# Raw weights of the down projection in three rings, and a reordered last norm, in a one-core decoder layer

## The chip, the core and the metric

The kernel runs on one core of a Trainium2 chip. TensorE (PE) multiplies matrices and takes its stationary operand by a separate weight load (PEld); VectorE (DVE) and ScalarE (ACT) work on tiles element by element; GpSimd (POOL) does little here; SyncE (SP) issues the transfers. The engines run at the same time, each its own instructions in a fixed order, and wait for one another by semaphores. The metric is the device time of one execution in microseconds (us): 1220.66 us is the median of three executions of the kernel before.

## What is computed

One layer of a decoder with two mixers side by side: a gated delta rule with four heads, and dilated sliding-window attention with eight heads; then one output projection, a residual, and a gated MLP with a short causal convolution. The sequence has 1024 positions, the model width is 1024, the MLP width 2816. Only the end of it bears on this change:

```python
x = x + jnp.concatenate([o_a, o_b], axis=-1) @ w_out
h = rmsnorm(x, norm2_w)
u = causal_dwconv(h @ w_up, ffn_conv_w)
gate, up = u[..., :D_FF], u[..., D_FF:]
x = x + (jax.nn.silu(gate) * up) @ w_down
...
return rmsnorm(x, final_norm_w)

def rmsnorm(x, w):
    y = xf * lax.rsqrt(jnp.mean(xf * xf, axis=-1, keepdims=True) + EPS)
    return (y * w.astype(jnp.float32)).astype(x.dtype)
```

The kernel holds x transposed: 1024 features as eight tiles of 128 partitions, positions along the free axis. A mean over features is therefore a sum over the eight tiles and over the partitions.

## The kernel before

**Products.** Operands are split in a high and a low part of a reduced-width float32 type (`F32R`), and every product of 128x128 by 512 is three matrix multiplications (`mm3`: high by high, high by low, low by high). The high part is an ACT copy, the low part a DVE subtraction (`split_block`).

**The MLP.** `mlp_up` runs over 22 channel tiles n. Both projections use a recursive scheme with seven products in place of eight (`up_product`, P1 to P7 on the way up). Between products ACT copies partial sums out of the bank `pa` while PE goes on adding to it: `p1`, then `u2` (a tile of the ring `wlo`), then `u3`, then `xu`. The activation of each channel tile is stored in DRAM (`upark`).

**The down projection** (`mlp_down`, and `prep` for operands) has four stages of eleven steps j. A step of stages 0, 1 and 2 has two operand pairs (e = 0 on the four banks `pa`, e = 1 on the four banks `pb`), 24 multiplications of 512 columns; a step of stage 3 has one pair on `pa`, 12 multiplications. When a stage ends, DVE adds its eight finished banks to the residual tiles `x1h` (`add_to`, table `ADDS`), while PE already starts on the same banks for the next stage; a bank can be written again only when its add is done. The `pa` banks come first in each step, then `pb`. From stage 2's end on, `complete` squares finished rows on ACT and sums the squares of the eight tiles into `rstdB` on DVE.

`prep` for a step issues the loads of raw weights (`wd`, 512 KB, or `wa`, 256 KB) and of activations (`r1`, `r2`, from `upark`), combines them on DVE and splits them. The raw tiles lie in pools named by a tag, a ring of two buffers each:

| stage | raw weights in | others |
|---|---|---|
| 0 | `wst` and `whi` in turn | |
| 1 | `wd` in `wst`, `wa` in `whi` | `t2` (a difference of activations) in `wlo` |
| 2 | `wst` and `whi` | |
| 3 | `wst` and `whi` in turn | |

The split operands (`pr`) go round eleven tags. All transfers of the kernel are issued by SP, in one order. In the up projection `wst` and `whi` hold raw up weights and `wlo` holds `u2`.

**The tail.** The last five steps of stage 3 are done bank by bank in two halves of 256 positions (`last_product(i, sl)`): four left banks, then the right banks. `final_norm` makes the last norm of a part: multiplications of `rstdB` with ones sum over partitions (`ss`), a scalar operation, a power on POOL (`rsqrt`), transpositions that spread the result over partitions (`pb`), and eight DVE multiplications, each followed by a store of a tile. The norm of the left half is started behind the first right bank; its eight multiplications stand on DVE ahead of the adds of the last two right banks.

**What sets the order.** The order on PE is written out: the generators of a `Weave` yield until their operands are ready by a cost estimate, and each product gets a token that keeps the order. On the other engines a scheduler orders instructions by priorities and estimated times; `uv` and `ua` are DVE and ACT at raised priority, `after(inst, anchor)` forces one instruction behind another. So another ring or another wait can move DVE, ACT and SP instructions that the diff doesn't touch. In the compiled kernels the order on PE and POOL is the same but for the added products, and those of DVE, ACT and SP differ from the end of the up projection on.

In the profile L139 is the helper through which all engine operations but products pass, L189 the multiplications of `mm`, L193 the transpositions of `tp`.

Of the kernel before, what the change touches and what calls it, by code (L numbers as in the profile page):

```python
# [7 lines left out]
F32 = mybir.dt.float32  # L8
F32R = mybir.dt.float32r
AF = mybir.ActivationFunctionType  # L10
OP = mybir.AluOpType
# [4 lines left out]
P = 128  # L16
# [8 lines left out]
EPS = 1e-6  # L25
# [119 lines left out]
def hybrid_layer(tc, I, out):  # L145
    nc = tc.nc
    wv = Weave()
    ve = Engine(wv, nc.vector, "vector", 0.07, 0.00105)
    ac = Engine(wv, nc.scalar, "scalar", 0.12, 0.00085)

    uv = Engine(wv, nc.vector, "vector", 0.07, 0.00105, first=tc.high_priority)
    ua = Engine(wv, nc.scalar, "scalar", 0.12, 0.00085, first=tc.high_priority)
    po_ = Engine(wv, nc.gpsimd, "gpsimd", 0.15, 0.0021)
    sy = Engine(wv, nc.sync, "sync", 0.05, 0.00142, 2.2)
    es = ExitStack()
    cp = es.enter_context(tc.tile_pool(name="cp", bufs=1))
# [6 lines left out]
    def tile_(pool, shape, dt, name, tag, bufs):  # L163
        return wv.slot(pool.tile(list(shape), dt, name=name, tag=tag, bufs=bufs), tag, bufs)
# [20 lines left out]
    def after(inst, anchor, reason="keeps a slot free until it is needed"):  # L185
        tc.add_manual_dep(inst.ins, anchor.ins.name, order, reason=reason)

    def mm(dst, lhs, rhs, us, start=True, stop=True, **kw):
        tc.stamp_issue_order_token(nc.tensor.matmul(dst, lhs, rhs, start=start, stop=stop, **kw).ins, TOKEN)  # L189
        wv.product(us, dst, lhs, rhs)  # L190

    def tp(dst, src, idt=None, us=0.11):
        tc.stamp_issue_order_token(nc.tensor.transpose(dst, src, ident if idt is None else idt).ins, TOKEN)  # L193
        wv.product(us, dst, src)
# [43 lines left out]
    def rsqrt(dst, src, n):  # L238
        po_.tensor_tensor(dst, src, mhalf[:, :n], op=OP.pow)
# [14 lines left out]
    def bank(tag, name="ps"):  # L254
        return tile_(pp_, (P, 512), F32, name, tag, 2)
# [1094 lines left out]
    pcount = [0]  # L1350
    LAST = 5

    def raw_tile(name, tag, src, n=2):
        t = tile_(wp, [P, n, 512], F32, name, tag, 2)
# [29 lines left out]
    def prep(stage, j):  # L1384
        if stage == 0:

            g = raw_tile("wd", ("wst", "whi")[j % 2], wd_rows(j, 0))
            r = R1[j] = acts("r1", R1TAGS[j], j, 0)
            ops[stage, j] = list(zip(split_pair(g), split_pair(r)))
            q = R2[j] = A("r2", R2TAGS[j], shape=(P, 2, 512))  # L1390
            sy.dma_start(q[:, 0, :], upark[j][:, half(1)])
            ve.tensor_tensor(r[:, 0, :], q[:, 0, :], r[:, 0, :], op=OP.subtract)
        elif stage == 1:

            u = raw_tile("wd", "wst", wd_rows(j, 1))
# [5 lines left out]
            ve.tensor_tensor(u[:, 0, :], u[:, 1, :], a[:, 0, :], op=OP.subtract)  # L1401
            ve.tensor_tensor(t2, q[:, 1, :], r[:, 0, :], op=OP.subtract)
            w = split_pair(u)
            ops[stage, j] = [(w[0], split_one(t2)), (w[1], split_one(r[:, 0, :]))]
            ve.tensor_tensor(r[:, 1, :], r[:, 1, :], t2, op=OP.subtract)
        elif stage == 2:

            g = raw_tile("wd", "wst", wd_rows(j, 0))
            u = raw_tile("wd", "whi", wd_rows(j, 1))
            ve.tensor_tensor(g, g, u, op=OP.subtract)  # L1410
            ve.tensor_tensor(g[:, 1, :], g[:, 0, :], g[:, 1, :], op=OP.add)
            r = R2[j]
            ve.tensor_tensor(r[:, 0, :], r[:, 1, :], r[:, 0, :], op=OP.subtract)
            ops[stage, j] = list(zip(split_pair(g), split_pair(r)))
        else:

            a = raw_tile("wa", ("wst", "whi")[j % 2], wd_rows(j, 1)[:, 1:2], 1)
# [13 lines left out]
    def part(m, hh, sl):  # L1431
        return slice(512 * hh + sl.start, 512 * hh + sl.stop)

    def add_to(pd, m, hh, sl):
        x = x1h[m][:, part(m, hh, sl)]
        ve.tensor_tensor(x, x, pd[:, sl], op=OP.add)

    def complete(m, hh, sl):

        sp_ = part(m, hh, sl)  # L1440
        x = x1h[m][:, sp_]
        sq = tile_(sp, [P, 512], F32, "sq3", "t2", 2)
        ac.activation(sq[:, sl] if m else rstdB[:, sp_], x, AF.Square)
        if m:
            ve.tensor_tensor(rstdB[:, sp_], rstdB[:, sp_], sq[:, sl], op=OP.add)

    def final_norm(hh, sl, tags, between=None):
        n_ = (sl.stop - sl.start) // P
        ss = bank(tags[0])
        for c in range(n_):  # L1450
            o = 512 * hh + sl.start + c * P
            mm(ss[:, c:c + 1], rstdB[:, o:o + P], ones[:, :1], 0.215)
        rs = tile_(sp, [P, 4], F32, "rs3", "rs3", 2)
        ve.tensor_scalar(rs[:, :n_], ss[:, :n_], 1.0 / 1024, EPS, op0=OP.mult, op1=OP.add)
        rsqrt(rs[:, :n_], rs[:, :n_], n_)
        if between is not None:
            between()
        pb = bank(tags[1])
        for c in range(n_):
            tp(pb[:, c * P:(c + 1) * P], rs[:, c:c + 1].to_broadcast([P, P]))  # L1460
        for m in range(8):
            x = x1h[m][:, part(m, hh, sl)]
            ve.scalar_tensor_tensor(x, x, fw[:, m:m + 1], pb[:, :sl.stop - sl.start], op0=OP.mult, op1=OP.mult)
            sy.dma_start(out[m * P:(m + 1) * P, part(m, hh, sl)], x)
# [6 lines left out]
    def mlp_down():  # L1471
        yield from wv.until("up")
        whole = slice(0, 512)
        pa = [bank(t, "dw") for t in ("asc", "atr") for _ in range(2)]
        pb = [bank(t, "dw") for t in ("hf", "ch") for _ in range(2)]
        def down_step(stage, j):
            for e, (op, pds) in enumerate(zip(ops[stage, j], (pa, pb))):
                for i in range(4):
                    down(pds[i], i, op, whole, j == 0 and (stage == 0 or (stage, e) == (1, 1)), j == HT - 1)
                if j == HT - 1:  # L1480
                    mg, hh = ADDS[stage][e]
                    for i in range(4):
                        add_to(pds[i], 4 * mg + i, hh, whole)
                        if stage == 0 and e == 1:
                            complete(i, 0, whole)
                        if stage == 2 and e == 1:
                            complete(i, 1, whole)
                    if stage == 2 and e == 1:
                        for i in range(4):
                            complete(4 + i, 1, whole)  # L1490

        for n, (stage, j) in enumerate(STEPS):
            if n + 1 < len(STEPS):
                prep(*STEPS[n + 1])
            if n in XLOADS:
                load_x1(*XLOADS[n])
            if stage == 3 and j == HT - LAST - 1:
                final_norm(1, whole, ("hf", "ch"), lambda: down_step(stage, j))
            elif stage < 3 or j < HT - LAST:
                down_step(stage, j)  # L1500

        def last_product(i, sl):
            for j in range(HT - LAST, HT):
                down(pa[i], i, ops[3, j][0], sl, False, j == HT - 1)
            add_to(pa[i], 4 + i, 0, sl)
            complete(4 + i, 0, sl)
# [12 lines left out]
    wv.add(1, gates())  # L1519
# [69 lines left out]
```

## Time and profile before

| what | us |
|---|---|
| median of three executions | 1220.66 (1220.21 to 1220.72) |
| the profiled execution, whole | 1219.28 |
| its span, first to last instruction | 1217.5 |
| PE busy | 1200.4 |
| DVE busy | 946.1 |
| ACT busy | 574.6 |

Mean granted TensorE clock in the profiled execution: 0.996 of full speed. In the time lines a row gives the start, the duration, the engine, the line, the operation with output and inputs, the count of merged instructions, and in brackets the idle time ahead and what ended it. A row of waits gives the total, the number and the longest. A row of a windows table for one engine gives the stretch, its length, the busy time, the granted clock, the share of the DMA engines and GB/s; without a choice of engine it has busy times for PE, PEld, DVE, ACT and POOL in this order. A row of DMA issues gives the count, the size and the us from issue to landing; the row of one tensor's instructions gives the shortest, median and longest issue in ns.

### The profile page before, as it was taken

The numbers are of one execution on the slowest core, as the hardware profiler recorded it, in microseconds if no ns is written. First come the engines' busy times: TensorE is split into PE (matmuls) and PEld (weight loads), VectorE is DVE, ScalarE is ACT, GpSimd is POOL, SyncE is SP. The second block draws the span as 40 slices with busy tenths as digits, with TensorE's granted clock in tenths as the row PEclk, the third lists the DMA queues.
The fourth block names the chain that finished last, engine by engine and source line by source line (L and its number), as shares of the span: only waits on it lengthen the run. The fifth ranks groups of instructions, "written<-read, shape, count | busy, mean of one in ns | idle before, by whom it ended". The sixth has DMA issues, their size and how long they took to land.

```text
span 1217.5 us, 18285 instructions
## 1 busy us (share of the span) xinstructions
PE 1200.4 (99%) x7064; PEld 986.3 (81%) x7064; DVE 946.1 (78%) x1459; ACT 574.6 (47%) x1124; POOL 52.1 (4%) x46
## 2 busy tenths in 40 slices
PE   9999999999999999999999999999999999999996
PEld 7878887889777778888888888888888888787886
DVE  7675965566477686767989988989889889899875
ACT  7393344356344453655544544445444444344441
POOL 0311010003100000000000000000000000000000
PEclk9999999999999999999999999999999999999998
DMA  7425252335634213444213223132231496555623
GB/s 231 107 79 165 83 145 85 116 127 164 214 102 129 88 36 107 173 139 144 82 57 105 68 88 104 52 104 68 89 104 53 141 376 234 165 177 177 181 87 139
DMA packets 85799, 154.81 MB, mean 127 GB/s; under 512 B 21168, under 2 KB 36304, under 8 KB 85712
## 3 DMA queue, kind: packets, MB, share of 16 engines
q1 hardware_dynamic: 85712, 153.64, 39.4%
q8 instruction: 55, 0.90, 0.3%
q14 instruction: 32, 0.26, 0.1%
HBM read 117.68 MB, written 35.93 MB: 126 GB/s over the span
## 4 chain that ended last, share of the span: by engine, by line
PE 87%; DVE 6%; DMA 3%; issue 2%; ACT 2%; SPq 0%; POOLq 0%; POOL 0%; DVEq 0%; ACTq 0%
PE ps L189 44%; PE pa L189 20%; PE pc L189 10%; PE dw L189 10%; PE ps L193 3%; DMA wd<-in_wd 2%; DVE pr L139 2%; DVE x1h L139 1%; DVE wd L139 1%; DVE kT L139 1%; ACT dec L139 1%; PE warm L189 1%; DVE wlo L139 0%; DMA r<-upark 0%; ACT sq L141 0%
## 5 line engine op out<-in xcount | busy, mean ns | idle before, releaser
L189 PE MATMUL dw<-pr 128*128 128x512 f32 (+1 forms) x984 | 213.0, 377 | 2.2 <-DVE x1h L139 2.2
L189 PEld LDWEIGHTS dw<-pr 128*128 128x128 f32 x984 | 176.1, 188 | 38.0 <-DVE x1h L139 4.4
L189 PE MATMUL ps<-xhi,whi 128*128 128x512 f32 x384 | 158.5, 413 | 0.0
L189 PE MATMUL ps<-xhi,wlo 128*128 128x512 f32 x384 | 150.3, 391 | 0.0
L189 PE MATMUL ps<-xlo,whi 128*128 128x512 f32 x384 | 150.1, 391 | 0.0
L189 PE MATMUL pa<-T,pair 128*128 128x512 f32 x528 | 127.1, 389 | 0.0
L189 PEld LDWEIGHTS pa<-T,pair 128*128 128x128 f32 x528 | 99.0, 188 | 20.5
L189 PEld LDWEIGHTS ps<-xhi,wlo 128*128 128x128 f32 x384 | 72.1, 188 | 15.7 <-DVE wlo L139 0.2
L189 PEld LDWEIGHTS ps<-xhi,whi 128*128 128x128 f32 x384 | 72.3, 188 | 14.9 <-issue 1.4
L189 PEld LDWEIGHTS ps<-xlo,whi 128*128 128x128 f32 x384 | 72.4, 189 | 12.1 <-DVE xlo L139 0.3
L139 ACT ACTIVATE u<-pa 128x512 f32<-128x512 f32 x44 | 26.3, 599 | 109.5 <-PE pa L189 109.5
L139 ACT ACTIVATE whi<-wst 128x1024 fp32r<-128x1024 f32 (+2 forms) x41 | 41.9, 1021 | 73.8 <-PE ps L189 65.9
L139 DVE SCALAR_TENSOR_TENSOR y<-xu,fcw,y 128x1023 f32<-128x1023 f32 (+1 forms) x44 | 56.3, 1281 | 22.1 <-ACT y L139 22.0
L141 ACT ACTIVATE sm<-sm,mx 128x128 f32<-128x128 f32 (+7 forms) x64 | 35.4, 555 | 60.0 <-DVE mx L141 60.0
L189 PE MATMUL pa<-T,S 128*128 128x512 f32 x264 | 63.4, 389 | 0.0
L189 PE MATMUL pa<-B,A 128*128 128x512 f32 x264 | 63.4, 389 | 0.0
L189 PE MATMUL pc<-T,S 128*128 128x512 f32 x264 | 63.4, 389 | 0.0
L189 PE MATMUL pc<-B,pair 128*128 128x512 f32 x264 | 63.4, 389 | 0.0
L139 DVE TENSOR_TENSOR wst<-wst 128x512 f32<-128x512 f32 x88 | 60.5, 687 | 0.9
L189 PE MATMUL ps<-B,pair 128*128 128x512 f32 x252 | 60.5, 389 | 0.0
L139 ACT ACTIVATE pr<-wd 128x1024 fp32r<-128x1024 f32 x33 | 34.9, 1058 | 50.5 <-DVE wd L139 28.0
L139 DVE TENSOR_TENSOR wlo<-wst,whi 128x1024 fp32r<-128x1024 f32 (+2 forms) x41 | 48.2, 1175 | 13.1 <-ACT whi L139 13.1
(245 smaller groups left out, 2360.9 us busy)
## 6 DMA issues: line engine op xcount, KB each, us to landing
wst<-in_wu SPq DMA_DIRECT2D x44, 512.0 KB, 3.7
wd<-in_wd SPq DMA_DIRECT2D x44, 512.0 KB, 4.3
upark<-y SPq DMA_DIRECT2D x22, 512.0 KB, 3.7
wst<-in_wi SPq DMA_DIRECT2D x21, 512.0 KB, 3.7
r<-upark SPq DMA_DIRECT2D x11, 512.0 KB, 7.9
r<-upark SPq DMA_DIRECT2D x22, 256.0 KB, 7.0
wa<-in_wd SPq DMA_DIRECT2D x22, 256.0 KB, 2.7
wst<-in_wv SPq DMA_DIRECT2D x8, 512.0 KB, 3.5
```

The costliest lines, as they stand in the source:

```text
L139: return getattr(eng, op)(*a, **kw)
L141: return getattr(eng, op)(*a, **kw)
L189: tc.stamp_issue_order_token(nc.tensor.matmul(dst, lhs, rhs, start=start, stop=stop, **kw).ins, TOKEN)
L193: tc.stamp_issue_order_token(nc.tensor.transpose(dst, src, ident if idt is None else idt).ins, TOKEN)
```

## The change

1. Every raw weight tile of the down projection takes the next of three tags, `wst`, `whi`, `wlo`, in turn, in all four stages. In stage 1 the 256 KB load fills one half of such a tile and `t2` is written to the other half.
2. `final_norm` is cut in three: `mean_of`, `turned`, `scale_out`. In the tail the left half's eight multiplications are spread: four, then the third right bank's add, three, then the fourth bank's add, one; `after` keeps them in this order. The fourth bank's square isn't added to `rstdB` by DVE; its partitions are summed by two more multiplications with ones, which add to the same bank as those of `rstdB`.
3. The last eight stores are issued by SP and ACT in turn.

```diff
+    sa = Engine(wv, nc.scalar, "actq", 0.05, 0.00142, 2.2)
...
+    def wd_tile(name="wd"):
+        wcount[0] += 1
+        return tile_(wp, [P, 2, 512], F32, name, ("wst", "whi", "wlo")[wcount[0] % 3], 2)
+
+    def raw_tile(src):
+        t = wd_tile()
         sy.dma_start(t, src)
...
-            g = raw_tile("wd", ("wst", "whi")[j % 2], wd_rows(j, 0))
+            g = raw_tile(wd_rows(j, 0))
...
-            u = raw_tile("wd", "wst", wd_rows(j, 1))
-            a = raw_tile("wa", "whi", wd_rows(j, 0)[:, 0:1], 1)
+            u = raw_tile(wd_rows(j, 1))
+            both = wd_tile("wa")
+            sy.dma_start(both[:, 0, :], wd_rows(j, 0)[:, 0, :])
...
-            t2 = tile_(wp, [P, 512], F32, "t2", "wlo", 2)
+            t2 = both[:, 1, :]
...
+        if apart:
+            return sq
         if m:
             ve.tensor_tensor(rstdB[:, sp_], rstdB[:, sp_], sq[:, sl], op=OP.add)
...
+    def mean_of(hh, sl, tag, more=None):
+        n_ = (sl.stop - sl.start) // P
+        ss = bank(tag)
+        for src, o in ((rstdB, 512 * hh + sl.start), (more, sl.start)):
+            if src is not None:
+                for c in range(n_):
+                    mm(ss[:, c:c + 1], src[:, o + c * P:o + c * P + P], ones[:, :1], 0.215,
+                       src is rstdB and (c == 0 or more is None), src is more or more is None, skip_group_check=True)
+        rs = tile_(sp, [P, 4], F32, "rs3", "rs3", 2)
+        uv.tensor_scalar(rs[:, :n_], ss[:, :n_], 1.0 / 1024, EPS, op0=OP.mult, op1=OP.add)
+        rsqrt(rs[:, :n_], rs[:, :n_], n_)
+        return rs
...
+    def scale_out(hh, sl, pb, ms=range(8), queues=(sy,), anchor=None):
+        for m in ms:
+            x = x1h[m][:, part(m, hh, sl)]
+            inst = ve.scalar_tensor_tensor(x, x, fw[:, m:m + 1], pb[:, :sl.stop - sl.start], op0=OP.mult, op1=OP.mult)
+            if anchor is not None:
+                after(inst, anchor, "the sums of the last banks go first")
+            queues[m % len(queues)].dma_start(out[m * P:(m + 1) * P, part(m, hh, sl)], x)
...
-        final_norm(0, left, ("hf", "ch"), lambda: last_product(1, right))
-        for i in (2, 3):
-            last_product(i, right)
-        final_norm(0, right, ("hf", "ch"))
+        rs = mean_of(0, left, "hf")
+        last_product(1, right)
+        pl = turned(rs, left, "ch")
+        scale_out(0, left, pl, range(0, 4))
+        third, _ = last_product(2, right)
+        scale_out(0, left, pl, range(4, 7), anchor=third)
+        fourth, more = last_product(3, right)
+        scale_out(0, left, pl, range(7, 8), anchor=fourth)
+        scale_out(0, right, turned(mean_of(0, right, "hf", more), right, "ch"), queues=(sy, sa))
```

More of the change, by code (lines that the diff above doesn't have):

```diff
@@ L1435, in add_to, with complete @@
         x = x1h[m][:, part(m, hh, sl)]
-        ve.tensor_tensor(x, x, pd[:, sl], op=OP.add)
-    def complete(m, hh, sl):
+        return ve.tensor_tensor(x, x, pd[:, sl], op=OP.add)
+    def complete(m, hh, sl, apart=False):
         sp_ = part(m, hh, sl)
@@ L1443, in complete @@
         ac.activation(sq[:, sl] if m else rstdB[:, sp_], x, AF.Square)
+        if apart:
+            return sq
         if m:
             ve.tensor_tensor(rstdB[:, sp_], rstdB[:, sp_], sq[:, sl], op=OP.add)
-    def final_norm(hh, sl, tags, between=None):
[L1448 to L1455, printed above, removed]
+    def mean_of(hh, sl, tag, more=None):
[10 more added lines that the diff above has]
+        return rs
@@ new lines, in turned @@
+    def turned(rs, sl, tag):
+        pb = bank(tag)
+        for c in range((sl.stop - sl.start) // P):
+            tp(pb[:, c * P:(c + 1) * P], rs[:, c:c + 1].to_broadcast([P, P]))
+        return pb
+    def scale_out(hh, sl, pb, ms=range(8), queues=(sy,), anchor=None):
[5 more added lines that the diff above has]
+            queues[m % len(queues)].dma_start(out[m * P:(m + 1) * P, part(m, hh, sl)], x)
@@ L1456, in final_norm @@
+    def final_norm(hh, sl, tags, between=None):
+        rs = mean_of(hh, sl, tags[0])
         if between is not None:
             between()
[L1458 to L1464, printed above, removed]
+        scale_out(hh, sl, turned(rs, sl, tags[1]))
@@ L1504, in last_product @@
                 down(pa[i], i, ops[3, j][0], sl, False, j == HT - 1)
-            add_to(pa[i], 4 + i, 0, sl)
-            complete(4 + i, 0, sl)
+            added = add_to(pa[i], 4 + i, 0, sl)
+            return added, complete(4 + i, 0, sl, sl.start > 0 and i == 3)
         left, right = slice(0, 256), slice(256, 512)
```

12 lines of the change are left out of this document (6 added, 6 removed).

## The prediction

> **What bounds the kernel now.** I read the page first, then who waited for whom from the down projection on, then time lines around the waits.
>
> ```profile
> span 1217.5 us, 18285 instructions
> PE 1200.4 (99%) x7064; PEld 986.3 (81%) x7064; DVE 946.1 (78%) x1459; ACT 574.6 (47%) x1124; POOL 52.1 (4%) x46
> ```
> ```profile
> PE dw L189 <- DVE x1h L139: 2.2, 5, 0.6
> ```
>
> The kernel is bound by its list of matrix products; the change adds two tiny ones and removes none. It can therefore win only where PE stands still: in five waits for the adds of finished banks (`x1h`) and in the tail. The first set lies at the seams between stages 0 and 1 and between 1 and 2:
>
> ```profile
> 850.18 5.44 PE pa L189 x24
> ```
> ```profile
> 1045.64 4.51 PE L189 MATMUL dw<-pr 128*128 128x512 f32 x19
> 1050.76 0.96 PE L189 MATMUL dw<-pr 128*128 128x512 f32 x3 [0.61 <-DVE x1h L139]
> 1051.96 3.06 PE L189 MATMUL dw<-pr 128*128 128x512 f32 x12 [0.23 <-DVE x1h L139]
> 1055.55 4.83 PE L189 MATMUL dw<-pr 128*128 128x512 f32 x20 [0.53 <-DVE x1h L139]
> 1105.78 7.19 PE L189 MATMUL dw<-pr 128*128 128x512 f32 x31
> 1113.36 3.06 PE L189 MATMUL dw<-pr 128*128 128x512 f32 x12 [0.39 <-DVE x1h L139]
> 1116.89 3.48 PE L189 MATMUL dw<-pr 128*128 128x512 f32 x14 [0.47 <-DVE x1h L139]
> ```
>
> One product takes 5.44/24 = 0.2267 us. From start to start the lost time is larger than the idle column: 1045.64 + 19 x 0.2267 = 1049.95, and the next starts at 1050.76 (0.81 lost); then 0.52 and 0.87; at the second seam 0.55 and 0.81. Together 3.56 us: 2.20 and 1.36.
>
> **Why the adds are late.** DVE makes the next operands and does the adds in one order.
>
> ```profile
> 988.70:1047.69 58.99, 51.76 (x60) 1.00 0.71 248
> 1047.69:1109.09 61.40, 57.55 (x82) 1.00 0.58 189
> ```
> ```profile
> DVE wd L139 <- DMA wd<-in_wd: 6.0, 3, 2.7
> ```
> ```profile
> DVE wd L139 <- DMA wd<-in_wd: 3.2, 5, 1.3
> ```
> ```profile
> 1047.69 1.28 DVE L139 TENSOR_TENSOR x1h<-x1h,dw 128x512 f32<-128x512 f32 x2
> 1048.88 1.22 DVE L139 TENSOR_TENSOR pr<-wd,pr 128x1024 fp32r<-128x1024 f32 x1
> 1050.02 0.68 DVE L139 TENSOR_TENSOR x1h<-x1h,dw 128x512 f32<-128x512 f32 x1
> ```
>
> In the first stretch DVE was idle for 58.99 - 51.76 = 7.2 us, 6.0 of them waiting for raw weights; between the seams 3.8 us, 3.2 for weights. The first add came at 1047.69. PE wanted that bank again at 1049.95 - 2 x 0.68 = 1048.59 and had left it 21 products before, at 1043.8. From there on each late add of the eight shifts PE.
>
> **Part 1, three rings.** Each ring has two buffers. Raw loads get six buffers instead of four; a step of stage 1 or 2 takes two of them, so loads can run three steps ahead of their use instead of two. Bytes and instructions are the same; t2 moves into the free half of its step's second buffer, at no price, since its write and readers are the same ones.
>
> First seam, from the compiled order of the changed kernel. ACT now copies `xu` ahead of the split of step 1's activations:
>
> ```profile
> 987.13 1.06 ACT L139 ACTIVATE pr<-r 128x1024 fp32r<-128x1024 f32 x1 [4.67 <-DMA r<-upark]
> 988.09 0.58 ACT L139 ACTIVATE xu<-pa 128x512 f32<-128x512 f32 x1
> ```
>
> PE ended that bank at 983.30 + 12 x 0.2267 = 986.0 (row below), so the copy and DVE's work behind it start 1.2 us or more earlier (I count 1.2). Up to the first add DVE has 3.0 us more to do, deeper preparation (0.60 us per 512-wide and 1.14 per 1024-wide instruction between starts, as 1047.69, 1048.88 and 1050.02 above show). Of the 7.0 us of waits (the rest are gaps) I expect 3 to stay: 2 for step 1's activations, which sit behind one more weight load in SP's queue, and 1 for a weight whose buffer comes free late. The first add comes at 1047.69 - 1.2 + 3.0 - 4.0 = 1045.5. The new order then gives the adds of the four `pa` banks at 1045.5, 1046.7, 1048.4 and 1049.6 and the last `pb` add at 1053.2; with 0.68 + 0.06 to finish, only the last is late (1053.9 against 1048.59 + 7 x 0.68 = 1053.35): 0.6 us left of 2.20.
>
> Second seam: 61.4 us of the same work lie between the first adds, less perhaps 2.3 of waits, so 1104.6. But the new order puts three preparing instructions (2.9 us) between the first and second add, one of them behind a load that may take another 1 us. PE wants the second bank at 1048.59 + 0.6 + 264 x 0.2267 + 0.68 = 1109.7; the add is done at 1108.8 to 1109.8, and the last `pb` add 0.35 to 1.2 late. I take 0.8 left of 1.36. Part 1 gives 3.56 - 1.4 = 2.2 us; bounds: all 3.56, or nothing.
>
> What the rings cost: the third ring's buffers also hold `u2` in the up projection. Step 1's load now waits for channel tile 20's `u2`, and ACT splits it ahead of its copy of the bank that PE writes next (`u3`):
>
> ```profile
> 974.88 0.38 SPq L139 DMA_DIRECT2D wd<-in_wd  x1
> ...
> 978.05 1.07 ACT L139 ACTIVATE pr<-wd 128x1024 fp32r<-128x1024 f32 x1 [1.02 <-PE pc L189]
> 980.77 0.60 ACT L139 ACTIVATE u<-pa 128x512 f32<-128x512 f32 x1 [1.65 <-PE pa L189]
> 983.30 2.88 PE L189 MATMUL pa<-T,pair 128*128 128x512 f32 x12
> ```
> ```profile
> wd<-in_wd SPq DMA_DIRECT2D x1, 512.0 KB, 4.3
> ```
> ```profile
> wd<-in_wd SPq DMA_DIRECT2D x1, 512.0 KB, 8.6
> ```
>
> The two landing times are those of the weight loads issued at 974.88 and 987.79. The new place of step 1's load is one short issue after 974.88; 975.5 + 4.3 to 5.5 is at most 981.0, the split 1.07, the copy 0.60: done by 982.7, 0.6 us before PE writes that bank at 983.30. I cost it at nothing, covered by that margin; if the load lands as late as the second row says, the price is 975.5 + 8.6 + 1.67 - 983.3 = 2.5 us. Step 4's load waits for tile 21's `u2` (near 991.6) and holds up the queue behind it by up to 4 us; its operand is wanted at 988.7 + 4 x 5.44 = 1010.5, so this lands on DVE's lead only.
>
> **Part 2, the tail.**
>
> ```profile
> 1199.04 0.61 PE L189 MATMUL ps<-ones,rstdB 128*128 128x1 f32 x4
> 1199.68 0.16 DVE L139 TENSOR_SCALAR rs<-ps 128x2 f32<-128x2 f32 x1 [0.30 <-PE ps L189]
> 1201.52 3.83 PE L189 MATMUL dw<-pr 128*128 128x256 f32 x30
> 1201.92 3.22 DVE L139 SCALAR_TENSOR_TENSOR x1h<-x1h,fw,ps 128x256 f32<-128x256 f32 x8
> 1205.39 0.74 DVE L139 TENSOR_TENSOR x1h<-x1h,dw 128x256 f32<-128x256 f32 x2
> 1205.89 0.75 ACT L139 ACTIVATE sq<-x1h 128x256 f32<-128x256 f32 x2 [3.38 <-DVE x1h L139]
> 1207.44 0.98 PE L189 MATMUL ps<-ones,rstdB 128*128 128x1 f32 x4 [2.10 <-DVE rstdB L139]
> 1208.54 0.16 DVE L139 TENSOR_SCALAR rs<-ps 128x2 f32<-128x2 f32 x1 [1.24 <-PE ps L189]
> 1210.26 3.22 DVE L139 SCALAR_TENSOR_TENSOR x1h<-x1h,fw,ps 128x256 f32<-128x256 f32 x8 [1.56 <-PE ps L193]
> ```
>
> Now eight multiplications (0.39 apart) stand before the last two adds, although the products end at 1205.35. In the new order: four from 1201.92, one sum at 1203.48, third add 1203.82, three multiplications to 1205.31, the third square's sum, fourth add at 1205.65 instead of 1205.71, the eighth multiplication behind it. So the adds themselves hardly move. What goes is the last sum on DVE: ACT's last square (0.50 after its add) ends at 1206.57; the ones take it directly, and the older sum's ones run earlier, in the shadow. From the ones to the scalar operation on `rs` it is 0.64 behind busy PE (1199.04 to 1199.68) and 1.10 here, behind 2.10 us of idle PE (1207.44 to 1208.54; the same four products take 0.98 instead of 0.61). In the new order PE is idle for half a us only.
> Starting near 1206.65 puts `rs` at 1207.3 to 1207.75. I take 1207.4, nearer the first, because the idle time before it is nearer to that row's: 1.1 us gained, between 0.8 and 1.25. Power, turning and first multiplication follow as now (1208.54 to 1210.26). Two more ones products are in these numbers.
>
> **Part 3, shared issue.** DVE ends its last multiplication at 1213.48, SP issues the last store at 1214.14, since its issues are 0.48 apart against 0.39:
>
> ```profile
> 1213.65 0.87 SPq L139 DMA_DIRECT2D out_xT<-x1h  x2
> 1213.00:1214.00 1.00, 0.00 (x0) 0.00 (x0) 0.48 (x2) 0.00 (x0) 0.00 (x0) 0.50 0.81 267
> ```
> ```profile
> L139 SPq DMA_DIRECT2D out_xT<-x1h x24: 332/392/1070, 1190.8 to 1214.1; - x24
> ```
>
> ACT has nothing left but these four issues, which stand behind its last square. Two issuers can follow DVE, so the last issue moves up by 0.55. No ACT issue is in the trace. By the slowest SP issue, 1.07, ACT's four would end 0.85 later than DVE allows and cost 0.3; by the median nothing. I take 0.55, since four issues of 0.39 fit easily. A rate cap is the third rival. On this the Trainium skill ("DMA: Bandwidth & Descriptors", "Issuing engines are not separate DMA queues") says that all issuers share 16 engines and only issue time is saved; by that alone the last landing would follow the first issue and this part would give 0. The row shows the engines busy 0.81 at 267 GB/s; DVE's pace needs 335, which is about 1.0.
>
> **Sum.** 2.2 + 1.1 + 0.55 = 3.85 us. The profiled execution took 1219.28 (span 1217.5 and 1.8 around it), which becomes 1215.4; the median of the three runs is 1.4 above it, 1220.66, and becomes **1216.8**.
>
> **Rivals.** *The seams stay*: the split tiles, not raw buffers, limit DVE's lead, or the deeper preparation ahead of the adds eats what the waits gave (3.0 us more before the first seam). Speaking for it: DVE has 57.55 of 61.40 us busy there. Then parts 2 and 3 alone: 1219.0, no change. *The stores are capped*: at 267 GB/s eight of 131 KB need 3.9 us, part 3 gives nothing, 1217.4. *Slower*: the loads held behind the one waiting for `u2` bring DVE to the seams later than now. Each us of lateness is paid at both seams; being 2 us later than now at each, against the 2.2 earlier that I get, gives 1220.66 + 4.0 - 1.65 = 1223.0. From 1 us later on it cancels the tail. For it: the load at 987.79 took 8.6 us to land; against it: 991.6 + 8.6 is 1000.2, 10 us ahead of its use at 1010.5.
>
> **How the numbers follow.** My forecast 0.52, capped stores 0.11 (both faster by over 0.2%, 2.44 us, about what a measurement tells from nothing), the seams stay 0.21, slower 0.16. My case runs from 1215.2 (all of 3.56 and 1.9 in the tail) to 1218; the range reaches to 1220.3 to take in the staying seams.
>
> **What would show it.** Right: waits of PE for `x1h` under 1 us in all, DVE's waits for `wd` loads halved, ones on the last square starting about 1.3 us after the last product, stores ending with DVE's pace. Wrong: a PE wait before 1045, above all near 983 or 999; DVE's first adds not earlier than 1047; ACT issues of 1 us.

## Result and profile after

The changed kernel takes 1217.10 us (median of eight executions, 1215.28 to 1217.97), the kernel before 1220.61 us on the same chip (1217.41 to 1221.32). The ratio is 0.997, with a 95% interval of 0.9961 to 0.9979. The profiled execution took 1215.28 us with a span of 1213.5 us; before, it was 1219.28 and 1217.5.

One sentence ahead of the prediction is not right: `complete` squares finished rows not only from stage 2's end on, but also four tiles of them at the end of stage 0.

The page's head of the changed kernel, and its row of the added queue (in this kernel L190 are the products and L194 the transpositions):

```profile
span 1213.5 us, 18279 instructions
PE 1199.5 (99%) x7068; PEld 985.4 (81%) x7068; DVE 945.3 (78%) x1458; ACT 574.3 (47%) x1124; POOL 51.7 (4%) x46
...
q10 hardware_dynamic: 576, 0.52, 0.1%
```

PE is still the bound; the 0.52 MB of q10 are the four stores that ACT now issues. From the down projection on, PE waits like this (changed kernel, the list of waits from 988 to 1206 us):

```profile
PE dw L190 <- DVE x1h L139: 1.4, 3, 0.7
PE ps L190 <- DVE rstdB L139: 0.6, 1, 0.6
PE ps L190 <- ACT sq L139: 0.2, 1, 0.2
```

The waits for `x1h` are 1.4 us in place of 2.2. PE's time line at both seams (two windows), changed kernel:

```profile
1039.83 10.38 PE L190 MATMUL dw<-pr 128*128 128x512 f32 x45
1050.38 3.01 PE L190 MATMUL dw<-pr 128*128 128x512 f32 x12 [0.17 <-DVE x1h L139]
1053.97 6.21 PE L190 MATMUL dw<-pr 128*128 128x512 f32 x26 [0.58 <-DVE x1h L139]
...
1099.69 14.97 PE L190 MATMUL dw<-pr 128*128 128x512 f32 x63
1115.32 5.07 PE L190 MATMUL dw<-pr 128*128 128x512 f32 x21 [0.66 <-DVE x1h L139]
```

By starts, the first seam loses 0.35 us (1039.83 + 45 x 0.2267 = 1050.03) and 0.87 us, together 1.22 in place of 2.20. The second loses 1.35 us (1099.69 + 63 x 0.2267 = 1113.97), as much as the 1.36 of before. And this is DVE at the first seam, with the waits ahead of it in the first rows:

```profile
DVE pr L139 <- ACT pr L139: 3.0, 2, 2.9
DVE wd L139 <- DMA wd<-in_wd: 1.9, 1, 1.9
```
```profile
1045.51 0.68 DVE L139 TENSOR_TENSOR x1h<-x1h,dw 128x512 f32<-128x512 f32 x1
1046.11 0.69 DVE L139 TENSOR_TENSOR wd<-wd,wa 128x512 f32<-128x512 f32 x1
1046.71 0.68 DVE L139 TENSOR_TENSOR x1h<-x1h,dw 128x512 f32<-128x512 f32 x1
1047.31 1.22 DVE L139 TENSOR_TENSOR pr<-wd,pr 128x1024 fp32r<-128x1024 f32 x1
1048.44 0.68 DVE L139 TENSOR_TENSOR x1h<-x1h,dw 128x512 f32<-128x512 f32 x1
1049.04 0.69 DVE L139 TENSOR_TENSOR pr<-wa,pr 128x512 fp32r<-128x512 f32 x1
1049.64 2.47 DVE L139 TENSOR_TENSOR x1h<-x1h,dw 128x512 f32<-128x512 f32 x4
```

DVE waits 1.9 us for raw weights where it waited 6.0, and comes to the first add at 1045.51, not 1047.69. But a preparing instruction stands behind each of the first three adds, so the third comes only 1.6 us earlier than before (1048.44 against 1050.02).

The tail of the changed kernel:

```profile
1199.94 3.83 PE L190 MATMUL dw<-pr 128*128 128x256 f32 x30
1204.09 0.42 DVE L139 TENSOR_TENSOR x1h<-x1h,dw 128x256 f32<-128x256 f32 x1
1204.32 0.58 PE L190 MATMUL ps<-ones,rstdB 128*128 128x1 f32 x4 [0.55 <-DVE rstdB L139]
1204.60 0.42 ACT L139 ACTIVATE sq<-x1h 128x256 f32<-128x256 f32 x1 [1.43 <-DVE x1h L139]
1205.07 0.61 PE L190 MATMUL ps<-ones,sq 128*128 128x1 f32 x4 [0.17 <-ACT sq L139]
1205.78 0.16 DVE L141 TENSOR_SCALAR rs<-ps 128x2 f32<-128x2 f32 x1 [0.89 <-PE ps L190]
1206.77 0.43 PE L194 MATMUL ps<-ident,rs 128*128 128x128 f32 x2 [1.10 <-POOL rs L139]
1207.24 3.22 DVE L139 SCALAR_TENSOR_TENSOR x1h<-x1h,fw,ps 128x256 f32<-128x256 f32 x8 [1.30 <-PE ps L194]
1208.15 2.69 ACTq L139 DMA_DIRECT2D out_xT<-x1h  x4
```

The last product ends at 1199.94 + 3.83 = 1203.77. Cut at the same events, the two profiled executions differ as follows:

| stretch, us | before | after | gain |
|---|---|---|---|
| start to first product of the down projection | 988.74 | 988.07 | 0.67 |
| first product to end of the last one | 216.61 | 215.70 | 0.91 |
| last product to scalar operation on `rs` | 3.19 | 2.01 | 1.18 |
| scalar operation to first multiplication | 1.72 | 1.46 | 0.26 |
| first multiplication to end of span | 7.24 | 6.26 | 0.98 |

No row ahead of the down projection shows work that the change took away, and its start differs from execution to execution: over ten profiles of this study (without the one with the moved turn, below) it lies between 988.07 and 989.97, with two rings (988.74 to 989.97) as with three. So I don't count the first row as the change's. The other rows are the seams (0.91) and the tail (2.42).

### The profile page after: what moved, and what is told of

It reads as the page before. It is cut to its first block, busy times and chain, and to the rows that moved or that the text cites. A ratio compares the mean times of both kernels' runs of the same rounds, so it can differ in the third digit from the quotient of the medians.

```text
span 1213.5 us, 18279 instructions
## 1 busy us (share of the span) xinstructions
PE 1199.5 (99%) x7068; PEld 985.4 (81%) x7068; DVE 945.3 (78%) x1458; ACT 574.3 (47%) x1124; POOL 51.7 (4%) x46
## 4 chain that ended last, share of the span: by engine, by line
PE 86%; DVE 7%; DMA 2%; issue 2%; ACT 2%; SPq 0%; POOLq 0%; POOL 0%; DVEq 0%; ACTq 0%
PE ps L190 44%; PE pa L190 20%; PE dw L190 10%; PE pc L190 10%; PE ps L194 3%; DVE pr L139 2%; DMA wd<-in_wd 1%; DVE x1h L139 1%; DMA r<-upark 1%; DVE kT L139 1%; DVE r L139 1%; DVE wd L139 1%; ACT dec L139 1%; DVE wlo L139 0%; DVE y L139 0%
## 5 line engine op out<-in xcount | busy, mean ns | idle before, releaser
L190 PE MATMUL dw<-pr 128*128 128x512 f32 (+1 forms) x984 | 212.9, 377 | 1.4 <-DVE x1h L139 1.4
L190 PEld LDWEIGHTS dw<-pr 128*128 128x128 f32 x984 | 176.2, 188 | 37.1 <-DVE x1h L139 3.5
L190 PE MATMUL ps<-xhi,whi 128*128 128x512 f32 x384 | 158.5, 413 | 0.0
L190 PE MATMUL ps<-xlo,whi 128*128 128x512 f32 x384 | 150.1, 391 | 0.2 <-DVE xlo L139 0.2
L190 PE MATMUL ps<-xhi,wlo 128*128 128x512 f32 x384 | 150.2, 391 | 0.0
L190 PE MATMUL pa<-T,pair 128*128 128x512 f32 x528 | 127.0, 389 | 0.0
L190 PEld LDWEIGHTS pa<-T,pair 128*128 128x128 f32 x528 | 99.0, 188 | 20.6
L190 PEld LDWEIGHTS ps<-xhi,wlo 128*128 128x128 f32 x384 | 72.1, 188 | 15.7 <-DVE wlo L139 0.2
L190 PEld LDWEIGHTS ps<-xhi,whi 128*128 128x128 f32 x384 | 72.2, 188 | 14.9 <-issue 1.4
L190 PEld LDWEIGHTS ps<-xlo,whi 128*128 128x128 f32 x384 | 72.4, 189 | 12.3 <-DVE xlo L139 0.6
L190 PE MATMUL pa<-B,A 128*128 128x512 f32 x264 | 63.4, 389 | 0.0
L190 PE MATMUL pc<-B,pair 128*128 128x512 f32 x264 | 63.4, 389 | 0.0
L190 PE MATMUL pc<-T,S 128*128 128x512 f32 x264 | 63.4, 389 | 0.0
L190 PE MATMUL pa<-T,S 128*128 128x512 f32 x264 | 63.4, 389 | 0.0
L190 PE MATMUL ps<-B,pair 128*128 128x512 f32 x252 | 60.5, 389 | 0.0
L139 ACT ACTIVATE pr<-r 128x1024 fp32r<-128x1024 f32 (+1 forms) x44 | 36.5, 839 | 49.0 <-PE dw L190 28.7
```

The costliest lines, as they stand in the source:

```text
L139: return getattr(eng, op)(*a, **kw)
```

## Experiments

My theory: the rings bring DVE earlier to the seams, and the tail gains by the sum that left DVE, by the spread multiplications and by two issuers, parts that simply add up. Rivals: only the tail counts; the rate of the transfers sets the end; the order of DVE's instructions, not the depth of the rings, is what costs at the seams. All ratios are against the kernel before on the same chip.

**The rings alone**, with the old tail and one issuer.

```diff
-        rs = mean_of(0, left, "hf")
-        last_product(1, right)
-        pl = turned(rs, left, "ch")
...
+        final_norm(0, left, ("hf", "ch"), lambda: last_product(1, right))
+        for i in (2, 3):
+            last_product(i, right)
+        final_norm(0, right, ("hf", "ch"))
```

> The changed kernel with the tail of the kernel before: rings alone. If the two profiles are read rightly, the seams lose 2.72 us instead of 3.56 and nothing else moves: about 0.8 us faster than before, 1219.8. If the prediction's term holds (2.2 us at the seams), 1218.4. If the 0.67 us by which the profiled products of the down projection started earlier also comes from the rings, 1.5 us faster, 1219.1. Last product to end of span about 12.15 us as before.

Measured: 1218.69 us, ratio 0.9986 (0.9977 to 0.9995), so 1.7 us by the ratio (0.6 to 2.8). In its profile PE waits 1.4 us for `x1h` and needs 215.80 us from first to last product; behind the last product it takes 12.09 us, as before (12.15). The rings gain something by themselves, and nothing in the tail; how much, of the 0.8, 1.5 and 2.2 us that I had named, the times do not tell.

**The tail and the shared issue alone**, with the two rings.

```diff
-            g = raw_tile(wd_rows(j, 0))
+            g = raw_tile("wd", ("wst", "whi")[j % 2], wd_rows(j, 0))
...
-            t2 = both[:, 1, :]
+            t2 = tile_(wp, [P, 512], F32, "t2", "wlo", 2)
```

> The kernel before with the changed tail and shared issue alone. By the two profiles 2.4 us faster than before, 1218.2, with 9.7 us from the last product to the end of the span instead of 12.15 and 3.56 us lost at the seams. By the prediction's terms 1.65 us, 1219.0.

Measured: 1218.25 us, ratio 0.9988 (0.9979 to 0.9997), 1.5 us (0.4 to 2.6). The profile is sharper: 9.68 us behind the last product, and 216.75 us between the first and the last, with waits of 2.2 us for `x1h` as in the kernel before. In these profiles the two halves of the change do not touch each other, and their gains together (1.7 + 1.5) are the change's 3.7 us (2.6 to 4.8) within what is measured.

**The additions first.** The changed kernel, with DVE's preparation of later weights forced behind the fourth add of a seam: the combinations of weights from step 3 of the next stage on, the splits from step 1 on.

```diff
+    def behind(inst, first):
+        if cur[1] >= first and cur[0] - 1 in seam:
+            after(inst, seam[cur[0] - 1], "the adds of the finished banks go first")
+        return inst
...
-        split_block(b, src)
+        behind(split_block(b, src)[1], 1)
...
-                        add_to(pds[i], 4 * mg + i, hh, whole)
+                        inst = add_to(pds[i], 4 * mg + i, hh, whole)
+                        if stage < 2 and (e, i) == (0, 3):
+                            seam[stage] = inst
```

> The changed kernel with DVE's preparation of the coming steps forced behind the fourth add of the first four banks at both seams. If the preparing instructions between the adds make the loss at the seams, PE's waits for x1h fall from 1.4 us to under 0.4 and the kernel is 2 to 2.7 us faster than the changed one, 1214.4 to 1215.1. If DVE's late arrival at the first add makes it, the first add stays where it is and at most 0.5 us is won. If the delayed preparation makes the next step's operands late, PE waits for pr instead and it is no faster or slower.

Measured: 1214.18 us (1213.24 to 1214.82), ratio 0.9951 (0.9939 to 0.9964). PE's waits and DVE's order, at the first seam with what follows, and at the second:

```profile
PE dw L190 <- DVE x1h L139: 0.2, 1, 0.2
```
```profile
1045.21 2.48 DVE L139 TENSOR_TENSOR x1h<-x1h,dw 128x512 f32<-128x512 f32 x4
1047.61 1.22 DVE L139 TENSOR_TENSOR pr<-wd,pr 128x1024 fp32r<-128x1024 f32 x1
```
```profile
1104.88 2.54 DVE L139 TENSOR_TENSOR x1h<-x1h,dw 128x512 f32<-128x512 f32 x4
```

Four adds in a row, and PE stops only once for `x1h`, for 0.2 us; from first to last product it takes 213.31 us, 2.39 less than in the changed kernel. Two things moved at once, though. No preparation stands between the four adds any more, and the combination that waited 1.9 us for its weights ahead of the first add now stands behind them, so the first add comes 55.67 us after the first product of the down projection, not 57.44. This run alone does not tell order from arrival; the next one does at the first seam.

**The same edit with the two rings**, on the kernel before.

> The kernel before, two rings, with the same forcing. If the order of the adds makes the loss, the four adds starting near 1047.7 in a row end by 1050.2 and most of the 3.56 us goes: 1217.3 to 1218. If the wait for raw weights makes it (the prediction's reason), the adds come as late as before and it stays within 0.7 us of 1220.6.

Measured: 1221.11 us, ratio 1.0005 (0.9996 to 1.0014): no gain, where I had expected one if the order makes the loss. The two seams went opposite ways. At the first, the four adds stand in a row, as late as in the kernel before (1047.70 for 1047.69), first DVE, then PE:

```profile
1047.70 2.47 DVE L139 TENSOR_TENSOR x1h<-x1h,dw 128x512 f32<-128x512 f32 x4
```
```profile
1043.80 9.19 PE L189 MATMUL dw<-pr 128*128 128x512 f32 x39
1053.16 9.17 PE L189 MATMUL dw<-pr 128*128 128x512 f32 x39 [0.18 <-DVE x1h L139]
```

PE loses 0.52 us there (1043.80 + 39 x 0.2267 = 1052.64), in place of 2.20. So at this seam the order did most of the work, with no earlier arrival. At the second seam, its DVE, and PE's waits for `x1h` at both:

```profile
1109.36 0.68 DVE L139 TENSOR_TENSOR x1h<-x1h,dw 128x512 f32<-128x512 f32 x1
1110.81 1.23 DVE L139 TENSOR_TENSOR wd<-wd 128x1024 f32<-128x1024 f32 x1 [0.78 <-DMA wd<-in_wd]
1111.95 0.68 DVE L139 TENSOR_TENSOR x1h<-x1h,dw 128x512 f32<-128x512 f32 x1
```
```profile
PE dw L189 <- DVE x1h L139: 2.8, 4, 1.2
```

All but 0.2 of these 2.8 us lie at the second seam, where the kernel before waits for less than 0.9. My edit lets the combinations of the next stage's first three steps pass; with four raw buffers the weights of one of them are still on their way when the adds are due, and the fourth add waits behind their load. Away from the seams PE loses another 1.1 us against the kernel before, and that is open. So the order pays without the deeper rings where the early weights are there in time, and this edit loses where they are late. Whether an edit that holds these combinations back too would gain with two rings was not run.

**One issuer again** for the last eight stores.

```diff
-        scale_out(0, right, turned(mean_of(0, right, "hf", more), right, "ch"), queues=(sy, sa))
+        scale_out(0, right, turned(mean_of(0, right, "hf", more), right, "ch"))
```

> The changed kernel with its last eight stores issued by SP alone again. The measure is the stretch from the end of the last product to the end of the span, 9.73 us in the changed kernel, because the down projection's start differs from run to run. If two issuers are worth what the prediction said (0.55 us, from the issue times), the stretch becomes 10.3 us; if they are worth all of what the stretch behind the first multiplication became shorter (7.24 before, 6.26 after), it becomes 10.7 us. The rival that the rate of the transfers sets the end, not the issue, says 9.7 us. Time against the changed kernel: 0.5 to 1.0 us more, or the same.

Measured: 1217.70 us, ratio 0.9978 (0.9969 to 0.9988). Behind the last product it takes 10.64 us, 0.91 more than the changed kernel, all of it behind the first multiplication (7.17 us). Over all profiles that stretch takes 7.17 to 7.60 us with one issuer (four) and 6.19 to 6.68 with two (six, with the same multiplications). Windows of 1 us without engine columns (stretch, length, granted clock, share of the DMA engines, GB/s) in the stores, first this kernel, then the changed one:

```profile
1212.00:1213.00 1.00, 0.50 0.81 267
```
```profile
1210.00:1211.00 1.00, 0.50 1.03 340
```

One issuer fills the DMA engines to 0.81, two to 1.03. 267 GB/s was no limit of the stores but SP's pace, and the rival of the capped transfers falls.

**The last square summed by DVE**, as before.

```diff
-            return added, complete(4 + i, 0, sl, sl.start > 0 and i == 3)
+            return added, complete(4 + i, 0, sl)
```

> The changed kernel with the last square added by DVE to the sum of the squares, as in the kernel before, instead of going to the ones as an operand of its own. The prediction's step says that the sum on DVE stands in the chain again: one addition and its hand-over, 0.5 to 0.65 us between the last square and the ones. PE would then also idle some 2.1 us before the ones, as before; if that idle time is what made the four ones products slow (0.98 us before, 0.61 after) and the two transposes (0.69 and 0.43), both rows return too, and the stretch from the last product to the end of the span grows from 9.73 to 10.8 us in all; if their length has another cause, to 10.3 us.

Measured: 1217.94 us, ratio 0.9984 (0.9975 to 0.9994). Behind the last product it takes 10.93 us, 1.20 more:

```profile
1204.94 0.42 DVE L139 TENSOR_TENSOR rstdB<-rstdB,sq 128x256 f32<-128x256 f32 x1 [0.15 <-ACT sq L139]
1205.52 0.58 PE L190 MATMUL ps<-ones,rstdB 128*128 128x1 f32 x4 [1.85 <-DVE rstdB L139]
1207.19 0.69 PE L194 MATMUL ps<-ident,rs 128*128 128x128 f32 x2 [1.10 <-POOL rs L139]
```

The scalar operation comes 0.52 later than in the changed kernel (2.53 against 2.01 behind the last product), which is the sum; the transpositions are back at 0.69 us, 0.26 later; another 0.42 lies behind the first multiplication (6.68 against 6.26), the largest of the six values with two issuers, for which I have no cause. The four ones products stayed at 0.58 us: the expected 0.98 did not return.

**The multiplications not spread**: all eight ahead of the last two adds.

```diff
-        scale_out(0, left, pl, range(0, 4))
+        scale_out(0, left, pl)
         third, _ = last_product(2, right)
-        scale_out(0, left, pl, range(4, 7), anchor=third)
         fourth, more = last_product(3, right)
-        scale_out(0, left, pl, range(7, 8), anchor=fourth)
```

> The changed kernel with the left half's eight multiplications in a row again, not spread behind the additions of the third and fourth bank sums. The prediction says that DVE's additions of the last two banks then wait behind multiplications of 0.42 us: the four multiplications that were moved back take 1.65 us of DVE, and the additions are due every 1.9 us, so the last addition comes 0 to 0.8 us later and the stretch from the last product to the end of the span is 9.7 to 10.5 us. The rival, that the spreading is the whole of the gain in the first part of the tail (1.18 us), says 10.9 us.

Measured: 1218.19 us, ratio 0.9985 (0.9976 to 0.9994); behind the last product 10.38 us, 0.65 more:

```profile
1203.89 3.83 PE L190 MATMUL dw<-pr 128*128 128x256 f32 x30
1207.76 0.75 DVE L139 TENSOR_TENSOR x1h<-x1h,dw 128x256 f32<-128x256 f32 x2
1208.72 0.42 DVE L139 TENSOR_TENSOR rstdB<-rstdB,sq 128x256 f32<-128x256 f32 x1 [0.21 <-ACT sq L139]
1209.29 0.58 PE L190 MATMUL ps<-ones,rstdB 128*128 128x1 f32 x4 [1.57 <-DVE rstdB L139]
```

The last add ends 0.79 us behind the last product (1203.89 + 3.83 = 1207.72); in the changed kernel it was 0.74. What the spreading gains is not the add but the third bank's square: unspread, its sum waits behind both adds, and the older ones with it. The scalar operation comes 2.7 us behind the last product, nearly the 2.8 of the rings alone: removing the sum from DVE is worth its full price only with the spreading.

**The turn of the rings moved by one**, so that step 0's raw tile is the one that waits for `u2`.

```diff
-    wcount = [0]
+    wcount = [1]
```

> The changed kernel with its turn of the three rings moved by one, so that the raw tile of the down projection's step 0 shares its buffers with the late up-projection copies and its load has to wait for them (step 1's did in the changed kernel, with 0.37 us to spare before PE). The slower rival of the prediction said that loads held behind a load that waits make PE wait at the start of the down projection, for up to 2.5 us; if that holds for the tile that is needed first, PE waits 0.5 to 2.5 us at the first products and the stretch from the down projection's first product to its last, or the gap before it, grows by that. If the waiting load is ahead of its use by as much as step 1's is, nothing grows by more than 0.3 us and the time stays within 0.5 us of the changed kernel's.

Measured: 1218.02 us, ratio 0.9979 (0.9969 to 0.9988). ACT and PE near the down projection's start:

```profile
982.01 1.06 ACT L139 ACTIVATE pr<-wd 128x1024 fp32r<-128x1024 f32 x1 [5.43 <-DMA wd<-in_wd]
...
984.87 0.58 ACT L139 ACTIVATE u<-pa 128x512 f32<-128x512 f32 x1
```
```profile
985.50 3.04 PE L190 MATMUL pa<-T,pair 128*128 128x512 f32 x12 [1.84 <-ACT u L139]
```

The mechanism of my slower rival is real: a split that waits for its weights holds up the copy behind it on ACT, and PE stands for 1.84 us. But the down projection, which started that much later (991.09), then needed only 214.61 us, with waits of 0.7 us at the seams. That DVE and the loads went on while PE stood would explain it, but 214.61 lies within the spread of the table below, so one profile does not show it. On the whole it is not told apart from the changed kernel (0.997, 0.9961 to 0.9979).

**Weight of the norm on ACT**, on top of the additions first: ACT multiplies the right residual tiles by the norm's weight while the mean is worked out.

```diff
+        rs = mean_of(0, right, "hf", more)
+        for m in range(8):
+            x = x1h[m][:, part(m, 0, right)]
+            ac.activation(x, x, AF.Copy, scale=fw[:, m:m + 1])
...
+            ve.tensor_tensor(x, x, pr[:, :256], op=OP.mult)
```

> e6_adds_first (additions ahead of the preparation at both seams) with the right half's last multiplications taken apart: ACT multiplies the residual tiles by the norm's weight while the mean is worked out, and DVE then multiplies two PSUM operands' worth less: a plain product of the tile and the factors. Theory of the seams: their loss stays as small as in e6 (PE waits 0.2 us in all, 213.3 us from the down projection's first product to its last, where five profiles with the rings alone lie between 214.5 and 217.9), because the order no longer lets a late load stand between the additions. Rival: e6's profile was one of the lucky ones, and the stretch is 214.5 us or more here. The tail: if DVE's multiplications set the end and a plain product is shorter, the stretch behind the last product is up to 0.4 us shorter than 9.65 us; if the stores set it, or the plain product takes as long (0.40 us), it stays 9.6 to 9.7 us.

Measured: 1214.15 us (1213.46 to 1214.48), ratio 0.994 (0.9926 to 0.9954), 213.33 us between first and last product, and 9.49 us behind it (9.65 with the additions first alone). So the seams' gain repeats, and the plain products take less:

```profile
1206.41 2.74 DVE L139 TENSOR_TENSOR x1h<-x1h,ps 128x256 f32<-128x256 f32 x8 [1.30 <-PE ps L194]
```

2.74 us in place of 3.22, of which 0.16 arrive at the end. By time the two versions can't be told apart; every execution of either is shorter than the shortest of the changed kernel (1215.28), though not all ran on one chip.

**How steady the seams are.** Five of these profiles have the changed kernel's instructions from the down projection's first product up to the tail, in the same order: the changed kernel, the rings alone, one issuer, the sum on DVE and the unspread multiplications. First add is counted from the down projection's first product; the third column is DVE's wait for raw weights from 1050 to 1108 us.

| kernel | first add | wait for weights | PE waits for `x1h` | first to last product |
|---|---|---|---|---|
| before | 58.95 | 3.2 | 2.2 | 216.61 |
| tail alone | 58.59 | 3.8 | 2.2 | 216.75 |
| after | 57.44 | 0.7 | 1.4 | 215.70 |
| rings alone | 57.43 | 0.6 | 1.4 | 215.80 |
| one issuer | 57.15 | 2.6 | 2.1 | 216.27 |
| sum on DVE | 56.54 | 0.5 | 0.9 | 214.54 |
| not spread | 57.98 | 2.7 | 3.4 | 217.88 |
| additions first, two rings | 58.85 | 3.6 | 2.8 | 218.08 |
| additions first | 55.67 | 0.7 | 0.2 | 213.31 |
| weight on ACT | 55.70 | 0.8 | 0.2 | 213.33 |

With the same instructions the stretch lies between 214.5 and 217.9. Where the weights between the seams came late (2.6 and 2.7 us), PE lost most. By seam (starts of the 30 products around each, less 0.2267 us for each, which counts the slower products behind a wait too), these five lose 0.5 to 2.0 us at the first, 1.3 in the mean, where the kernel before and the tail alone lose 2.3 and 1.7; at the second they lose 1.3 to 3.2, 2.0 in the mean, against 1.5 and 2.0. So what the rings gain, they gain at the first seam. Why the weights come late in some executions is open; and both profiles with three rings and the adds first had punctual weights, so how that order stands up to late ones is not seen.

## Why the prediction was right, and where not

The forecast, 1216.8 us, is 0.3 from the measured 1217.10, and faster by over 0.2% was the likeliest case. The terms of the sum did less well than the sum: they were 2.2 at the seams and 1.65 in the tail, and the profiles show 0.91 and 2.42. That 1.3 us too much and 0.8 us too little nearly cancel is luck. By my own signs, the waits for raw weights, the ones on the last square and the stores came out right; the waits of PE for `x1h`, which were to be under 1 us, are 1.4.

**Part 1 (2.2 us) was sized too high.** The direction and the mechanism hold: DVE's waits for raw weights fell from 6.0 to 1.9 us before the first seam and from 3.2 to 0.7 between the seams, and the adds came at the very times I gave (the first at 1045.51 for 1045.5, the fourth at 1049.64 for 1049.6). But PE came 0.67 us earlier in that execution, so counted from the down projection's start the first add was at 57.44 us, where I had 56.8. Over the five profiles it is 57.3 in the mean, against 58.8 with two rings: the rings move DVE by 1.5 us, not by 2.2. I had left DVE 3.0 us of waits before the first seam; it has 4.9, of which 2.9 is one wait for ACT's split, so that the terms of that time were not right and their sum is partly luck. My "only the last is late, 0.6 us left" became 0.35 for the fourth `pa` bank and 0.87 for the last `pb` bank. At the second seam I left 0.8; 1.35 stayed, nothing gained. The three preparing instructions between the first two adds stood in the prediction, with a load among them that may take longer: the second bank cost PE 0.2 us in this profile, but 1.1 and 1.9 us in the two with late weights (one issuer, not spread). The last `pb` add, which I had 0.35 to 1.2 late, cost 0.9 us in all five. By times the rings are worth 1.7 us (0.6 to 2.8), which still holds my 2.2; the mean of the five profiles, 216.04 against 216.68 with two rings (two profiles), says 0.6. What failed is the size, above all at the second seam, and that one profile was taken as if the loads came at the same time in each execution.

**Part 2 (1.1 us) was right in its steps, and its size is partly luck.** I had the fourth add 0.30 us behind the last product, the ones on the last square 1.30 and the scalar operation 2.05; the rows show 0.32, 1.30 and 2.01. "Power, turning and first multiplication follow as now" failed in my favour: 1.46 us in place of 1.72, since the transpositions ran at full clock. One reading behind it was wrong: I put the slow ones products of before (0.98 us) down to the 2.10 us that PE had idled. With the rings alone PE idles the same 2.10 us and they take 0.58; so 0.4 us of the 1.18 belong to that one execution of the kernel before. What the change itself earned there is 0.8, the low end of my 0.8 to 1.25. The whole tail is steadier: 12.15, 12.09 and 11.76 us behind the last product with the old one, 9.73, 9.68 and 9.65 with the new.

**Part 3 (0.55 us) was sized too low.** Undoing it costs 0.91. Against the kernel before, the last issue does move up by what I had (3.87 us behind the first multiplication, 3.26 after), and the other third of a us lies between the last issue and the end (3.4 and 3.0 us); in the run with one issuer it is all issue (4.19 us, and 3.0 to the end). ACT's issues take 0.34 to 0.38 us each, near SP's shortest, so the bound with issues of 1.07 was empty. On the Trainium skill's rule that all issuers share the same engines and only sequencer time is saved ("DMA: Bandwidth & Descriptors", "Issuing engines are not separate DMA queues"): the traces agree with the first half as far as they go: with two issuers the share of the 16 engines rises from 0.81 to 1.03, about full. I had read from it that the last landing follows the first issue and nothing is gained; it is the pace of issue that the end followed, and here that time was not small.

**What I costed at nothing** held, narrowly. In the changed kernel ACT's copy of `u3` ended at 981.68 + 0.58 = 982.26, PE wrote the bank at 982.63:

```profile
980.71 1.06 ACT L139 ACTIVATE pr<-wd 128x1024 fp32r<-128x1024 f32 x1 [4.34 <-DMA wd<-in_wd]
981.68 0.58 ACT L139 ACTIVATE u<-pa 128x512 f32<-128x512 f32 x1
```

0.37 us to spare where I had 0.6; in the seven profiles with that turn of the rings it is 0.37 to 1.01, and with the turn moved the price was 1.84 us of the 2.5 that I had given as its most.

**The rivals.** That the seams stay is refuted as a whole by the times of the rings alone, but it holds for the second seam (1.36 before, 1.35 after) and for some executions (217.88). The capped stores are refuted. Of the slower rival the first link was shown with the moved turn; that it brings DVE late to the seams was not: there DVE came earlier against PE than in the changed kernel.

## What to carry to other kernels

When adds of finished banks and preparation for later steps share one in-order engine, deeper buffers shorten its waits, but a scheduler may spend the lead on preparation between the adds; forcing the few instructions that PE waits for to the front was worth more than the buffers (2.4 us of profile against 0.9). Without the deeper buffers the same edit won at one seam and lost at the other, where it left early combinations free. For a tail, count the links behind the last product, and let TensorE sum what is still missing as an extra operand; where each store takes longer to issue than the work before it, give the stores two issuers. And price a term that hangs on loads from several executions: with the same instructions this stretch ranged over 3.3 us.

## What the runs showed of the hardware

How soon the granted clock fell after the last dense product differed from profile to profile. Windows of half a us of PE (stretch, length, busy, clock, DMA share, GB/s), the first of the kernel before, whose last product ended at 1205.35, the second of the changed kernel, 1203.77:

```profile
1207.35:1207.85 0.50, 0.41 (x2) 0.50 0.00 0
```
```profile
1208.77:1209.27 0.50, 0.00 (x0) 0.68 0.85 279
```

Before, the clock halved 2.0 us after the last product, with the rings alone and with the sum on DVE 2.6 us after it, with the additions first on two rings 3.4; with two rounds of ones that start within 2.1 us of it, in the changed kernel and six others, only 4.1 to 5.2 us after it, behind the transpositions. These took 0.43 us there and 0.69 in the four profiles where it had halved. It looks as if the small products put it off, but that is not shown. By the traces' clock records the stretch at full clock lasted 1201.49, 1204.90 or 1208.32 us in all eleven profiles, which is 352, 353 and 354 times 3.413 us: the clock falls on steps of 3.41 us, and where the last product lies within a step differs between executions. The step that ended with the halving in the kernel before still held 1.4 us of dense products; in the unspread kernel a step with 2.0 us of them and no ones was not followed by the halving. So the share of dense work in a step may explain all eleven, and whether ones count is open. The Trainium skill ("TensorE: Matmul & The Clock Gate", "What's actually happening") has the clock halved after an idle window of about 3.4 us that runs freely: the steps agree with its figure, and that the moment varies agrees, but the window that counted as idle in the kernel before was idle for 2.0 us only.

Whether a stall of PE far from the end is paid in full is not told here: with 1.84 us of it at the start of the down projection, the ratio was 0.9979 (0.9969 to 0.9988), without it 0.997 (0.9961 to 0.9979).
